# A two-layer encoder trunk on one core: attention in four steps, layer 1's first projections as Strassen-like quads, weights requested later

## The chip, the cores and the metric

The kernel runs on one core of a Trainium2 chip. The metric is the device time of one execution in microseconds (us). Engines: TensorE (PE), VectorE (DVE), ScalarE (ACT), GpSimd (POOL), and SyncE (SP), which here only issues transfers.

## What is computed

Two layers, each with a token mixer of two branches and a feed-forward block, on 1024 tokens of width 1024 in float32:

```python
for layer in range(2):
    hn = rmsnorm(h, norm1_g[layer])
    proj = hn @ w_in[layer]          # u 512, q 512, k 128, v 128, gate_a 1024, gate_b 1024
    y_a = s5_branch(u, ...)          # two-directional S5 scan (32 groups), gelu, z * sigmoid(z @ w_glu)
    y_b = windowed_gqa(q, k, v, ...) # blocks of 128 queries against 3 blocks of keys, a sink logit, T5 bias
    merged = sigmoid(gate_a) * (y_a @ w_branch_a[layer]) + sigmoid(gate_b) * (y_b @ w_branch_b[layer])
    h = h + merged @ w_out[layer]
    hn2 = rmsnorm(h, norm2_g[layer])
    h = h + (silu(hn2 @ w_gate[layer]) * (hn2 @ w_up[layer])) @ w_down[layer]
return rmsnorm(h, final_g)
```

## The kernel before

**Numbers.** Every operand of a large product is split into two float32r parts, `hi` (a cast, on ACT) and `lo` (the rest, a subtraction on DVE). A product of a 128x128 weight block with 512 tokens is three matmuls of PE: hi by hi, hi by lo, lo by hi (`chain`). A weight granule of 128x1024 comes by an SP transfer into one of four `raw` buffers and is then split (`whi` on ACT at L164, `wlo` on DVE at L165). Tokens are in two halves `h` of 512, so a 128-wide output tile of a projection (`proj`, PSUM bank `pj`) is two items of 24 matmuls, one for each half.

**Quads.** The feed-forward block takes gate and up tiles in pairs (`Quad`): sums and differences of the halves of the input (`sums`, `sum_pairs`: tiles `tt0` to `tt3`) and of the weights make seven products do the work of eight. A pair of plain tiles is 96 matmuls, a quad 84.

**Order.** The program is a list of items, `self.seq`, recorded by `build`; an item is a function and the granules it needs. `emit` runs it in order; `ahead` fetches and splits granules ahead of their use: before granule n is split, granules up to n + `R_BUFS` (4) are requested. Engines take instructions in the order of their queues; the order in a stretch of the start is strict, elsewhere a scheduler may move an instruction among its neighbours.

**Layer.** A layer goes through: the norm; projections k, v, q0, q1, u; 16 attention units (2 key heads x 8 blocks); the S5 stage; the gated unit on the S5 output (`glu`); the branches; w_out; the feed-forward block.

- *Attention* (`attention_items`). A unit is: scores into four banks `s` on PE (`att_scores`), with bias and maximum on DVE (`x<-s`, L797) and exponentials on ACT; scaling on DVE (`att_scale`, L814); transposes on PE (`att_transpose`, bank `pt`, L822), copied by ACT to `p`; products with v on PE (`att_values`, bank `pv`). In a loop of 18 steps, step i has the scores and scaling of unit i, the transposes of unit i-1 and the values of unit i-2. Filler items (projections not needed yet: q2, q3 and gate tiles) stand between them, `per` of them to a step: 0.6 in layer 0, 1 in layer 1.
- *S5* (`s5_states`, `s5_output`, `s5_gelu`, `s5_store`). There are 16 states and 8 outputs. A state is 16 matmuls (bank `s5x`), nine instructions of DVE (L949 to L965, four of them one scan each, the last ones make `s5s`), four copies on ACT to `s5sg` (L969). An output `s5y` takes two states; ACT squares and copies it, DVE makes `s5w`, ACT a tanh, DVE `s5g` (L1007), and four transfers take it to `zd` (L1012). Of the 16 states, 6 are made in the last attention steps; the loop of `s5_items` takes the rest, two to an iteration, with `per` fillers: 2.2 in layer 0, 2 in layer 1.
- *glu* (`glu_items`). Loads `z` back from `zd` in token order (L1097), splits it into `zp0` to `zp3`, and multiplies.

In layer 1 the filler list has 42 items: six of u, four of q2 and q3, and 32 of the gates. Its attention takes 20 of them, the S5 loop 18, and four stand between the S5 loop and glu. In layer 0 the fillers of the S5 loop are the seven gate items left by attention and the branch products `br` of attention's output (12 matmuls each).

Of the kernel before, what the change touches and what calls it, by code (L numbers as in the profile page):

```python
# [96 lines left out]
class Trunk:  # L97
# [582 lines left out]
    apart = None  # L680

    def proj(self, l, m, done, xs=None):

        g = self.w_in(l, m)
        apart = self.apart
        st = {}

        def half(h):
            def run(part=None):
                if part != 1:  # L690
                    st[h] = self.PS(f"pj{m}")
                self.chain(st[h], g, 0, (xs or self.hn)[h], part)
                if apart is None and part != 0:
                    done(h, st[h])
            return run
        if apart is not None:
            apart.extend([(lambda: done(0, st[0]),), (lambda: done(1, st[1]),)])
        return [(half(h), g) for h in range(2)]
# [75 lines left out]
    def att_scores(self, l, kv, b):  # L774
# [5 lines left out]
        sm = self.pm.tile([P, 4, 4], F32, tag="sm", name="sm", bufs=3)  # L780
# [85 lines left out]
    def attention_items(self, l, keys, q23, fill, per, tail):  # L866
# [3 lines left out]
        fill = (list(fill[:2]) if l else []) + q23 + list(fill[2 if l else 0:])  # L870
# [15 lines left out]
        for i in range(18):  # L886
            want = min(len(fill), round(per * (i + 1)) + max(0, i - 15))
# [15 lines left out]
            if i in (5, 7):  # L903
# [217 lines left out]

    def w_out_items(self, l):
# [48 lines left out]
    def ffn_items(self, l, fill, head):  # L1171
# [65 lines left out]
        def sums(j):  # L1237

            at = ((j, 0), (j, 1), (j + 4, 0), (j + 4, 1))
            if early:  # L1240
                y11, y12, y21, y22 = (ys.pop(a) for a in at)
            else:
                y11, y12, y21, y22 = (self.A("y") for _ in at)
                for y, (m, h) in zip((y11, y12, y21, y22), at):
                    hi, lo = self.hn2[h][m]
                    V.tensor_tensor(y, hi.bitcast(F32), lo.bitcast(F32), ADD)
            V.tensor_tensor(y11, y12, y11, SUB)
            V.tensor_tensor(y12, y22, y12, SUB)
            V.tensor_tensor(y22, y22, y11, SUB)
            V.tensor_tensor(y21, y21, y22, SUB)  # L1250
            for k, y in enumerate((y11, y22, y12, y21)):
                T[k][j] = (y, None)

        def sum_pairs(j, k):
            T[k][j] = self.split(T[k][j][0], f"tt{k}")

        def quad_items(f):

            q = Quad(self.t["w_gate"][l, f].rearrange("p k c -> p (k c)"), self.t["w_up"][l, f].rearrange("p k c -> p (k c)"))
            b = {}  # L1260

            def product(bank, g, off, xs, start):
                def run():
                    if start:
                        b[bank] = self.PS(f"q{bank}")
                    self.piece(b[bank], g, off, xs(), start)
                return (run, g)

            B = lambda h, a: lambda: self.hn2[h][a:a + 4]
            p = [product("x", q.a, 0, B(0, 0), True), product("y", q.b, HC, lambda: T[1], True),  # L1270
                 product("v", q.b, 0, lambda: T[0], True), product("x", q.a, HC, B(0, 4), False),
                 product("y", q.c, 0, lambda: T[2], False), product("w", q.d, 0, lambda: T[3], True),
                 product("v", q.e, 0, B(1, 4), False)]

# [103 lines left out]
    def build(self):  # L1378
# [31 lines left out]
        for l in range(DEPTH):  # L1410
# [23 lines left out]
            n0, n1 = (self.norm_parts(h, "ra", 2 * l, lambda m, h=h, src=src: src(m, h), lambda: self.hn) for h in range(2))  # L1434
            v1, v2 = self.halves(vc[0])
            loads, states = self.s5_head(l)
            tail_items = {11: pairs[:1] if l == 0 else []}
            for k, (ld, sts) in enumerate(zip(loads, states)):
                a = 18 - 2 * S5_LEAD + k
                tail_items.setdefault(a - 3, []).append(ld)  # L1440
                tail_items.setdefault(a, []).append(sts)
            if l == 0:
# [3 lines left out]
                def squares(h):  # L1446
                    for m in range(KT):
# [3 lines left out]
                va, vb = self.halves(vc[1])  # L1451
                qa, qb = self.halves(qc[1])
                self.add([(start_layer,), kc[0], vc[0], sq[0], kc[1], va, n0[0], sq[1], vb, n0[1], ke[0], ve[0], n1[0], n0[2],
                          qc[0], n0[3], n0[4], qa, n1[1], ke[1], ve[1], qe[0], qb, n0[5], n1[2], qe[1], q1[0], n1[3], scal[0],
# [9 lines left out]
            else:  # L1464

                k1, k2 = self.halves(kc[0])
# [24 lines left out]
            else:  # L1491
                left = self.s5_items(l, left, 2)
# [148 lines left out]
```

## Time and profile before

| | us |
|---|---|
| median of three runs (2645.35 to 2647.42) | 2646.05 |
| the profiled execution | 2647.46 |
| its span | 2645.7 |
| PE busy | 2589.6 |
| DVE busy | 1660.8 |
| ACT busy | 1066.1 |

The profiled execution is read below; its time is 1.4 us above the median and 1.8 us above its own span. "Busy" is the time in which an engine has an instruction in hand; matmuls overlap, so PE's pace is read from the distance between starts, not from the length of one. Stages of the span, by the names of the tiles that PE works on: layer 0's attention runs from about 213 to 372 us; its S5 stage to about 475; its feed-forward block to 1352; layer 1's norm and k, v, q from 1352 to 1412; its attention to 1598; its S5 stage to 1709; a run of fillers, then glu, to about 1765; the rest to 2645.7.

### The profile page before, as it was taken

The numbers are of one execution on the slowest core, as the hardware profiler recorded it, in microseconds if no ns is written. First come the engines' busy times: TensorE is split into PE (matmuls) and PEld (weight loads), VectorE is DVE, ScalarE is ACT, GpSimd is POOL, SyncE is SP. The second block draws the span as 40 slices with busy tenths as digits, with TensorE's granted clock in tenths as the row PEclk, the third lists the DMA queues.
The fourth block names the chain that finished last, engine by engine and source line by source line (L and its number), as shares of the span: only waits on it lengthen the run. The fifth ranks groups of instructions, "written<-read, shape, count | busy, mean of one in ns | idle before, by whom it ended". The sixth has DMA issues, their size and how long they took to land.

```text
span 2645.7 us, 35155 instructions
## 1 busy us (share of the span) xinstructions
PE 2589.6 (98%) x12878; PEld 2108.3 (80%) x12878; DVE 1660.8 (63%) x3333; ACT 1066.1 (40%) x2053; POOL 360.5 (14%) x524
## 2 busy tenths in 40 slices
PE   8999999999999999999999999999999999999997
PEld 6886677887788888888877778888878888888886
DVE  8985877575986745544673576546376644654556
ACT  5336744422443433333344553353235433333332
POOL 0131001000142210121010001100002221122010
PEclk9999999999999999999999999999999999999998
DMA  4353435354273652564332235434315652455253
GB/s 139 127 182 122 146 119 181 115 191 143 60 194 115 124 105 63 112 127 94 99 151 76 88 120 181 145 124 161 127 64 114 133 124 63 91 121 113 60 109 134
DMA packets 157438, 321.36 MB, mean 121 GB/s; under 512 B 20768, under 2 KB 55840, under 8 KB 157264
## 3 DMA queue, kind: packets, MB, share of 16 engines
q1 hardware_dynamic: 106192, 201.68, 23.3%
q0 software_dynamic: 51072, 117.43, 20.4%
q8 instruction: 101, 1.65, 0.3%
q14 instruction: 73, 0.60, 0.1%
HBM read 196.37 MB, written 122.63 MB: 121 GB/s over the span
## 4 chain that ended last, share of the span: by engine, by line
PE 92%; DVE 5%; issue 1%; ACT 1%; DMA 1%; POOL 1%; SPq 0%; DVEq 0%; POOLq 0%; ACTq 0%
PE pj L176 7%; PE pj L177 6%; PE pj L178 6%; PE dn L176 6%; PE dn L177 6%; PE dn L178 6%; PE qy L188 2%; PE qx L188 2%; PE qx L187 2%; PE qv L188 2%; PE qv L187 2%; PE qy L187 2%; PE qv L189 2%; PE qx L189 2%; PE qy L189 2%; PE br L176 2%
## 5 line engine op out<-in xcount | busy, mean ns | idle before, releaser
L165 DVE TENSOR_TENSOR wlo<-raw,whi 128x1024 fp32r<-128x1024 f32 (+3 forms) x210 | 186.6, 889 | 263.3 <-ACT whi L164 252.3
L164 ACT CAST whi<-raw 128x1024 fp32r<-128x1024 f32 (+3 forms) x210 | 164.3, 782 | 372.1 <-PE pj L177 125.0
L176 PE MATMUL pj<-rah,whi 128*128 128x512 f32 x768 | 306.9, 400 | 1.1 <-ACT rah L113 1.0
L177 PE MATMUL pj<-ral,whi 128*128 128x512 f32 x768 | 300.7, 392 | 0.8 <-DVE ral L114 0.8
L178 PE MATMUL pj<-rah,wlo 128*128 128x512 f32 x768 | 300.4, 391 | 0.0
L1218 POOL DMA_DIRECT2D hs<-dx x208 | 179.4, 868 | 846.6 <-ACT dx L1217 724.7
L176 PEld LDWEIGHTS pj<-rah,whi 128*128 128x128 f32 x768 | 144.8, 189 | 35.1 <-issue 2.4
L178 PEld LDWEIGHTS pj<-rah,wlo 128*128 128x128 f32 x768 | 144.8, 189 | 31.0
L177 PEld LDWEIGHTS pj<-ral,whi 128*128 128x128 f32 x768 | 144.9, 189 | 30.0 <-DVE ral L114 1.8
L1217 ACT COPY dx<-dn 128x512 f32<-128x512 f32 x208 | 121.1, 583 | 76.1 <-PE dn L178 75.4
L797 DVE CUSTOM_DVE_ANT_0 x<-s,bias,nsink 128x384 f32<-128x384 f32 (+1 forms) x128 | 67.7, 580 | 65.7 <-PE s L791 65.6
L187 PE MATMUL qx<-rfh,whi 128*128 128x512 f32 x280 | 108.9, 389 | 0.0
L188 PE MATMUL qx<-rfl,whi 128*128 128x512 f32 x280 | 108.9, 389 | 0.0
L189 PE MATMUL qx<-rfh,wlo 128*128 128x512 f32 x280 | 108.9, 389 | 0.0
L969 ACT COPY s5sg<-s5s 64x256 f32<-64x256 f32 x128 | 51.8, 405 | 123.6 <-DVE s5s L964 116.6
L176 PE MATMUL wo<-mgh,whi 128*128 128x512 f32 x256 | 100.0, 391 | 0.0
L178 PE MATMUL wo<-mgh,wlo 128*128 128x512 f32 x256 | 99.7, 389 | 0.0
L177 PE MATMUL wo<-mgl,whi 128*128 128x512 f32 x256 | 99.6, 389 | 0.0
L113 ACT CAST ffah<-ts 128x512 fp32r<-128x512 f32 x35 | 21.7, 621 | 190.1 <-DVE ts L1296 190.1
L176 PE MATMUL dn<-ffbh,whi 128*128 128x512 f32 x232 | 91.4, 394 | 0.0
L177 PE MATMUL dn<-ffbl,whi 128*128 128x512 f32 x232 | 90.6, 390 | 0.0
L177 PE MATMUL dn<-ffal,whi 128*128 128x512 f32 x232 | 90.4, 390 | 0.0
(431 smaller groups left out, 6711.2 us busy)
## 6 DMA issues: line engine op xcount, KB each, us to landing
hs<-dx POOLq DMA_DIRECT2D x208, 256.0 KB, 6.1
raw<-in_w_in SPq DMA_DIRECT2D x52, 512.0 KB
raw<-in_w_gate SPq DMA_DIRECT2D x44, 512.0 KB
raw<-in_w_up SPq DMA_DIRECT2D x44, 512.0 KB
raw<-in_w_down SPq DMA_DIRECT2D x96, 192.0 KB
g<-th POOLq DMA_DIRECT2D x64, 256.0 KB, 2.9
thr<-g SPq DMA_DIRECT2D x64, 256.0 KB
hs<-h POOLq DMA_DIRECT2D x48, 256.0 KB, 2.3
```

Of the source, the lines that this page charges most:

```text
L164: nc.scalar.copy(g.hi[:, :n], g.raw[:, :n])
L165: nc.vector.tensor_tensor(g.lo[:, :n], g.raw[:, :n], g.hi[:, :n].bitcast(F32), SUB)
L176: mm(ps, lhsT=wh, rhs=xh, start=k == 0, stop=False)
L177: mm(ps, lhsT=wh, rhs=xl, start=False, stop=False)
L178: mm(ps, lhsT=wl, rhs=xh, start=False, stop=k == n - 1)
L187: mm(ps, lhsT=wh, rhs=xh, start=start and k == 0, stop=False)
L188: mm(ps, lhsT=wh, rhs=xl, start=False, stop=False)
L189: mm(ps, lhsT=wl, rhs=xh, start=False, stop=k == len(xs) - 1)
L797: V.tensor_tensor_reduce(out=x[:, :n], in0=ps[:, :n], in1=self.bias[hd][:, bo:bo + n], op0=ADD, op1=ALU.min, scale=-1.0, scalar=self.nsink ...
L969: nc.scalar.copy(SG[64 * r:64 * r + 64, g * 256:(g + 1) * 256].rearrange("p (d n) -> p d n", d=2), Sv[64 * g:64 * g + 64, :, r])
L1217: nc.scalar.copy(t, ps)
L1218: nc.gpsimd.dma_start(self.hs[m, h], t, accum_op=ADD)
```

## The change

The main parts of the diff:

```diff
@@ ahead @@
-            self.fetch_to(min(self.split_ + R_BUFS, len(self.order)))
+            g = self.order[self.split_]
+            self.fetch_to(min(self.split_ + (R_BUFS if isinstance(g, QuadPart) else R_BUFS - 1), len(self.order)))
@@ att_scores @@
-        sm = self.pm.tile([P, 4, 4], F32, tag="sm", name="sm", bufs=3)
+        sm = self.pm.tile([P, 4, 4], F32, tag="sm", name="sm", bufs=4)
@@ attention_items @@
-        for i in range(18):
-            want = min(len(fill), round(per * (i + 1)) + max(0, i - 15))
+        for i in range(19):
+            want = min(len(fill), (min(i + 1, 3) + round(0.45 * max(0, i - 2)) if l == 0 else round(per * (i + 1))) + max(0, i - 15))
...
+            if 0 <= i - 3 < 16:
+                self.item(lambda u=i - 3: values(u))
             if 0 <= i - 2 < 16:
-                self.item(lambda u=i - 2: values(u))
+                self.item(lambda u=i - 2: transpose(u))
             if 0 <= i - 1 < 16:
-                self.item(lambda u=i - 1: transpose(u))
-            if i < 16:
-                self.item(lambda u=i: scale(u))
+                self.item(lambda u=i - 1: scale(u))
@@ linear_quads (new; sums, sum_pairs and quad_products are the code of the feed-forward block, now methods) @@
+        for (m1, done1), (m2, done2) in zip(tiles[::2], tiles[1::2]):
+            p, b = self.quad_products(self.t["w_in"][l, m1], self.t["w_in"][l, m2], lambda: self.hn, T)
...
@@ build, layer 0 @@
-                self.add([(start_layer,), kc[0], vc[0], sq[0], kc[1], va, n0[0], sq[1], vb, n0[1], ke[0], ve[0], n1[0], n0[2],
-                          qc[0], n0[3], n0[4], qa, n1[1], ke[1], ve[1], qe[0], qb, n0[5], n1[2], qe[1], q1[0], n1[3], scal[0],
+                self.add([(start_layer,), kc[0], vc[0], sq[0], kc[1], n0[0], sq[1], vc[1], n0[1], ke[0], ve[0], n1[0], n0[2],
+                          qc[0], n1[1], n0[3], ke[1], ve[1], qe[0], n0[4], qc[1], n0[5], n1[2], qe[1], q1[0], n1[3], scal[0],
@@ build, layer 1 @@
-                         [k1, n1[0], k2, v1, n1[1], n1[2], v2, n1[3], n1[4], n1[5], qc[0], ke[0], ve[0], qe[0], kc[1], ke[1],
-                          vc[1], ve[1]] + keys[:2] + [qc[1], qe[1], vals, bias0] + q1 + us[:2])
-                left = self.attention_items(l, keys, q23, us[2:] + gb + ga, 1, tail_items)
+                us = self.linear_quads(l, [lambda i=i: self.tile_u(l, i) for i in range(4)], T)
+                kvq = self.linear_quads(l, [lambda: self.tile_kv(l, M_K, kn), lambda: self.tile_kv(l, M_V, vn),
+                                            lambda: self.tile_q(l, 0), lambda: self.tile_q(l, 1)], T)
...
+                         [a[0], n1[0], a[1], c[0], n1[1], n1[2], c[1], n1[3], n1[4], n1[5], gb[4], *s[:2], gb[1], *s[2:], gb[3], *sp[1], gb[5],
+                          *sp[0], gb[6], *sp[2], gb[7], *sp[3]] + us + kvq[:15] + keys + kvq[15:17] + [vals] + kvq[17:] + [bias0])
+                left = self.attention_items(l, [None] * 4, q23, gb[8:] + ga, 0.9, tail_items)
...
             else:
-                left = self.s5_items(l, left, 2)
+                left = self.s5_items(l, left, 1)
```

So a plain granule is requested when three others, not four, stand before it; the attention loop has 19 steps, with the scaling of unit i-1, the transposes of unit i-2 and the values of unit i-3 in step i; in layer 0's start two halves of v and q are no longer cut and one norm step stands earlier; in layer 1 eight items of gate tiles (four tiles) go ahead, the sums of the normed input are made between them, and u, k with v, and q0 with q1 become four quads. The filler list of layer 1 then has 28 items, of which 0.9 go to an attention step and one to an S5 iteration.

Where rows are shown below they are the instructions in the order in which they stand in one engine's queue. The first place is PE in layer 0's attention: `s` are score banks, `x` the weights after DVE (L797 or L802 makes `x_2668` of `s_2662`, and `x_2657` of `s_2651`), `pt` the transposes. Before:

```order
L791 MATMUL s_2662<-kk00_2114,qn1_677 128x128
...
L822 MATMUL pt_2706<-cst_226,x_2561 128x128
...
L176 MATMUL pj7_2733<-rah_706,whi_2151 128x512
...
L791 MATMUL s_2761<-kk01_2117,qn1_677 128x384
...
L822 MATMUL pt_2801<-cst_226,x_2668 128x128
```

Now:

```order
L796 MATMUL s_2651<-kk00_2112,qn1_650 128x128
...
L827 MATMUL pt_2695<-cst_226,x_2504 128x128
...
L796 MATMUL s_2723<-kk01_2115,qn1_650 128x384
...
L827 MATMUL pt_2763<-cst_226,x_2558 128x128
...
L176 MATMUL pj10_2793<-rah_585,whi_2372 128x512
...
L796 MATMUL s_2829<-kk01_2115,qn1_650 128x384
...
L827 MATMUL pt_2869<-cst_226,x_2657 128x128
```

The transposes of a unit stood behind the scores of the next unit; now they stand behind those of the unit after that, so one more unit's scores, values and transposes lie between a unit's scores and its transposes.

The second place is PE in layer 1's S5 loop, from the output after states 12 and 13 to the end of the loop; each `pj` line is the first of 24 matmuls of a filler, each `s5y` the first of an output. Before:

```order
L983 MATMUL s5y<-s5uk 128x128
...
L941 MATMUL s5x<-s5uk,s5wbt 64x128 x8
L176 MATMUL pj_15560<-rah,whi 128x512
...
L941 MATMUL s5x<-s5uk,s5wbt 64x128 x8
L176 MATMUL pj_15629<-rah,whi 128x512
...
L983 MATMUL s5y<-s5uk 128x128
...
L176 MATMUL pj_15680<-rah,whi 128x512
...
L176 MATMUL pj_15718<-rah,whi 128x512
```

Now, from the output before the last two states:

```order
L988 MATMUL s5y<-s5uk 128x128
...
L946 MATMUL s5x<-s5uk,s5wbt 64x128 x8
L176 MATMUL pj_15993<-rah,whi 128x512
...
L946 MATMUL s5x<-s5uk,s5wbt 64x128 x8
L988 MATMUL s5y<-s5uk 128x128
...
L176 MATMUL pj_16081<-rah,whi 128x512
...
L988 MATMUL s5y<-s5uk 128x128
...
L176 MATMUL pj_16138<-rah,whi 128x512
...
L176 MATMUL glu<-zp0h,whi 128x512
```

An iteration with states had two fillers and has one; outputs without states stand behind one filler instead of two, and behind the last output there is one filler before glu.

The third place is ACT from the last output to glu; `th` is the tanh of a gate tile, `s5g<-s5w` the tanh of the last output, `zp` the split of glu's input. Before:

```order
L988 ACTIVATE s5g<-s5y 128x512
L989 COPY s5yc<-s5y 128x512
L768 ACTIVATE th_15794<-pj_15769 128x512
L1000 ACTIVATE s5g<-s5w 128x512
L164 CAST whi<-raw 128x1024
L768 ACTIVATE th_15832<-pj_15807 128x512
L768 ACTIVATE th_15866<-pj_15841 128x512
L164 CAST whi<-raw 128x1024
L768 ACTIVATE th_15901<-pj_15876 128x512
L113 CAST zp0h<-z_15905 128x512
```

Now:

```order
L993 ACTIVATE s5g<-s5y 128x512
L994 COPY s5yc<-s5y 128x512
L164 CAST whi<-raw 128x1024
L773 ACTIVATE th_16163<-pj_16138 128x512
L1005 ACTIVATE s5g<-s5w 128x512
L113 CAST zp0h<-z_16175 128x512
```

Three fillers less stand between the last output's tanh and the first split of glu's input; the tanh still stands behind the tanh of the filler that follows the output.

## Rows read from the trace of the kernel before

**Rows 1.** The page: span, and part 1, busy time of each engine.

```profile
span 2645.7 us, 35155 instructions
...
PE 2589.6 (98%) x12878; PEld 2108.3 (80%) x12878; DVE 1660.8 (63%) x3333; ACT 1066.1 (40%) x2053; POOL 360.5 (14%) x524
```

**Rows 2.** Timeline of PE, two fillers of layer 1: start, length, instruction.

```profile
1696.84 0.39 PE L176 MATMUL pj<-rah,whi 128*128 128x512 f32 x1
...
1707.04 0.38 PE L983 MATMUL s5y<-s5uk 128*128 128x128 f32 x2
...
1709.63 0.48 PE L176 MATMUL pj<-rah,whi 128*128 128x512 f32 x1
```

**Rows 3.** The page, part 5: a group of the feed-forward quads; last column: idle before.

```profile
L187 PE MATMUL qx<-rfh,whi 128*128 128x512 f32 x280 | 108.9, 389 | 0.0
```

**Rows 4.** Windows: length, busy us of PE, PEld, DVE, ACT, POOL; TensorE clock; DMA.

```profile
213.00:372.00 159.00, 145.89 (x961) 105.47 (x963) 116.94 (x383) 102.05 (x281) 14.76 (x27) 1.00 0.35 118
1598.00:1709.00 111.00, 111.00 (x704) 93.50 (x701) 77.93 (x156) 44.37 (x88) 22.79 (x39) 1.00 0.54 178
...
450.00:475.00 25.00, 19.21 (x112) 16.43 (x111) 19.62 (x42) 12.46 (x26) 4.76 (x8) 0.86 0.25 82
```

**Rows 5.** Waits of PE, 213 to 372 us: total, times, longest.

```profile
PE pt L822 <- DVE x L814: 3.1, 1, 3.1
PE pt L822 <- ACT th L768: 3.0, 1, 3.0
```

**Rows 6.** Timeline of PE at the start.

```profile
40.24 1.87 PE L303 MATMUL psn<-ones,sqa 128*128 128x1 f32 x8 [4.47 <-DVE sqa L294]
```

**Rows 7.** Timeline of DVE, one iteration of layer 1's S5 loop.

```profile
1665.22 0.69 DVE L949 TENSOR_TENSOR s5a<-s5x,s5tb 128x512 f32<-128x512 f32 x1
...
1671.91 0.69 DVE L949 TENSOR_TENSOR s5a<-s5x,s5tb 128x512 f32<-128x512 f32 x1 [1.20 <-PE s5x L941]
...
1677.31 0.68 DVE L999 SCALAR_TENSOR_TENSOR s5w<-s5g,s5yc 128x512 f32<-128x512 f32 x1
1678.44 1.23 DVE L165 TENSOR_TENSOR wlo<-raw,whi 128x1024 fp32r<-128x1024 f32 x1 [0.44 <-ACT whi L164]
1680.67 0.69 DVE L1007 SCALAR_TENSOR_TENSOR s5g<-s5g,s5yc 128x512 f32<-128x512 f32 x1 [1.01 <-ACT s5g L1000]
1681.30 0.69 DVE L949 TENSOR_TENSOR s5a<-s5x,s5tb 128x512 f32<-128x512 f32 x1
```

**Rows 8.** Timeline of ACT in the same iteration.

```profile
1677.36 1.05 ACT L164 CAST whi<-raw 128x1024 fp32r<-128x1024 f32 x1 [4.67 <-PE pj L177]
1678.31 1.68 ACT L969 COPY s5sg<-s5s 64x256 f32<-64x256 f32 x4
1680.01 0.63 ACT L1000 ACTIVATE s5g<-s5w 128x512 f32<-128x512 f32 x1
```

**Rows 9.** Timeline of PE in layer 0's S5 stage.

```profile
447.93 1.10 PE L941 MATMUL s5x<-s5uk,s5wbt 128*64 128x128 f32 x16
448.95 0.50 PE L176 MATMUL br<-ybh,whi 128*128 128x512 f32 x1
...
457.76 1.97 PE L941 MATMUL s5x<-s5uk,s5wbt 128*64 128x128 f32 x16 [5.79 <-DMA s5uk<-ud]
```

**Rows 10.** Timelines of ACT, DVE and SP behind the last S5 output.

```profile
1715.37 0.60 ACT L768 ACTIVATE th<-pj 128x512 f32<-128x512 f32 x1 [4.38 <-PE pj L178]
1715.86 0.62 ACT L1000 ACTIVATE s5g<-s5w 128x512 f32<-128x512 f32 x1
...
1717.24 2.46 SPq L1012 DMA_DIRECT2D zd<-s5g  x4
```

**Rows 11.** All instructions on tile `zd`: issue to landing; those on `z`: duration in ns.

```profile
DMA to landing us min/median/max: 2.0/2.7/5.8
...
L113 ACT CAST zp3h<-z x4: 607/627/635, 499.5 to 1755.2; 128x512 fp32r<-128x512 f32 x4
L114 DVE TENSOR_TENSOR zp3l<-z,zp3h x4: 684/684/693, 500.2 to 1756.1; 128x512 fp32r<-128x512 f32 x4
```

More of the change, by code (lines that the diff above doesn't have):

```diff
@@ L678, in w_in @@
         return Granule(self.t["w_in"][l, m].rearrange("p k c -> p (k c)"), DM)
-    apart = None
+    apart = grab = None
     def proj(self, l, m, done, xs=None):
+        if self.grab is not None:
+            self.grab.append((m, done))
+            return []
         g = self.w_in(l, m)
@@ L869, in attention_items @@
         stage = {}
-        fill = (list(fill[:2]) if l else []) + q23 + list(fill[2 if l else 0:])
+        fill = q23 + list(fill)
         def scores(u):
@@ L902, in attention_items @@
             self.add(tail.get(i, []))
-            if i in (5, 7):
+            if i in (5, 7) and keys[-1]:
                 self.add([keys[(i - 1) // 2]])
@@ L1119, in glu_items, with sums @@
         return early, split, out
+    def sums(self, T, ys, pairs, j):
+        V = self.nc.vector
+        at = ((j, 0), (j, 1), (j + 4, 0), (j + 4, 1))
+        if ys is not None:
+            y11, y12, y21, y22 = (ys.pop(a) for a in at)
+        else:
+            y11, y12, y21, y22 = (self.A("y") for _ in at)
+            for y, (m, h) in zip((y11, y12, y21, y22), at):
+                hi, lo = pairs[h][m]
+                V.tensor_tensor(y, hi.bitcast(F32), lo.bitcast(F32), ADD)
+        V.tensor_tensor(y11, y12, y11, SUB)
+        V.tensor_tensor(y12, y22, y12, SUB)
+        V.tensor_tensor(y22, y22, y11, SUB)
+        V.tensor_tensor(y21, y21, y22, SUB)
+        for k, y in enumerate((y11, y22, y12, y21)):
+            T[k][j] = (y, None)
@@ new lines, in sum_pairs, with quad_products, product, run @@
+    def sum_pairs(self, T, j, k):
+        T[k][j] = self.split(T[k][j][0], f"tt{k}")
+    def quad_products(self, src1, src2, pairs, T):
+        q = Quad(*(s.rearrange("p k c -> p (k c)") for s in (src1, src2)))
+        b = {}
+        def product(bank, g, off, xs, start):
+            def run():
+                if start:
+                    b[bank] = self.PS(f"q{bank}")
+                self.piece(b[bank], g, off, xs(), start)
+            return (run, g)
+        B = lambda h, a: lambda: pairs()[h][a:a + 4]
+        return [product("x", q.a, 0, B(0, 0), True), product("y", q.b, HC, lambda: T[1], True),
+                product("v", q.b, 0, lambda: T[0], True), product("x", q.a, HC, B(0, 4), False),
+                product("y", q.c, 0, lambda: T[2], False), product("w", q.d, 0, lambda: T[3], True),
+                product("v", q.e, 0, B(1, 4), False)], b
@@ L1237, in sums @@
         def sums(j):
[L1239 to L1252, printed above, removed]
+            self.sums(T, ys, self.hn2, j)
         def sum_pairs(j, k):
-            T[k][j] = self.split(T[k][j][0], f"tt{k}")
+            self.sum_pairs(T, j, k)
         def quad_items(f):
[L1259 to L1273, printed above, removed]
+            p, b = self.quad_products(self.t["w_gate"][l, f], self.t["w_up"][l, f], lambda: self.hn2, T)
             def first():
@@ L1433, in build @@
             src = (lambda m, h: xs[h][m]) if l == 0 else (lambda m, h: self.h2[m, h])
-            n0, n1 = (self.norm_parts(h, "ra", 2 * l, lambda m, h=h, src=src: src(m, h), lambda: self.hn) for h in range(2))
+            ys, T = {}, [[None] * 4 for _ in range(4)]
+            n0, n1 = (self.norm_parts(h, "ra", 2 * l, lambda m, h=h, src=src: src(m, h), lambda: self.hn, ys if l else None)
+                      for h in range(2))
             v1, v2 = self.halves(vc[0])
             loads, states = self.s5_head(l)
-            tail_items = {11: pairs[:1] if l == 0 else []}
+            tail_items = {12: pairs[:1] if l == 0 else []}
             for k, (ld, sts) in enumerate(zip(loads, states)):
-                a = 18 - 2 * S5_LEAD + k
+                a = 19 - 2 * S5_LEAD + k
                 tail_items.setdefault(a - 3, []).append(ld)
```

44 lines of the change are left out of this document (41 added, 3 removed).

## The prediction

> **What bounds the kernel now.** I read the page's busy line first [rows 1]: PE has an instruction in hand for 2589.6 of 2645.7 us, so the time is PE's work plus the places where PE waits, about 56 us by that line. Then PE's pace: from 1696.84 to 1707.04 us 45 matmuls of 512 columns start [rows 2], 0.2267 us each, though one lasts 0.39. A filler of 24 is 5.44 us, and the output `s5y` behind it takes 2.6 (1707.04 to 1709.63). So two kinds of edit can pay: fewer matmuls, or fewer waits. A third kind can cost: taking PE work out of a place where it hid another engine. For that I read the windows by stage [rows 4]. In layer 0's attention PE is busy 145.89 of 159 us, so 13.1 us are waits. In layer 1's S5 stage PE is busy all 111 us, so nothing waits there now; DVE is busy 77.9 of them, but not evenly, since only five of its eight outputs stand beside new states. Last come the timelines of DVE, ACT and SP at the places that the change touches.
>
> **Later requests.** In layer 0 and in the feed-forward blocks, SP's queue holds the same transfers in the same order as before, except for one `w_br_b` granule that moves behind six S5 loads. A request waits for the split that frees its buffer, and that is the same split. So I count nothing, also for the largest single wait of layer 0, 5.79 us for an S5 load [rows 9]. If it did go, about 8 us would be gained: the wait and half of some 4.4 us that PE then works at half clock (the window's clock is 0.86 [rows 4]).
>
> **The start.** PE waits 4.47 us for the sum of squares of half 1 [rows 6]. Two splits of a weight (1.2 us each, the length of `wlo` in [rows 7]) no longer stand ahead of these squares on DVE, so the sum can come about 2 us earlier; against it a norm step stands earlier and finds its sum less ready. DVE is the busy engine until half 1 is normed, and its work is not less. I take a gain of 2, between 0 and the 4.47 of the wait.
>
> **Four attention steps, layer 0.** The two largest waits are transposes waiting for DVE's `x` and for ACT to free a bank, 3.1 and 3.0 us [rows 5]. PE's own work for a unit is (145.89 - 13 fillers x 5.44 - 6 `s5x` x 1.02) / 16 = 4.3 us, DVE's (116.94 - 6 states x 5.4 - 7 splits x 1.2) / 16 = 4.8, with its tables. With one more unit between a unit's scores and its transposes, the chain maximum, exponential, scaling has 4.3 us more of PE work to hide behind. What is late next is DVE itself: in a step with a state it has 10.2 us of work, PE 5.3 and a filler of 5.44, and where the filler is missing DVE falls behind. Walking the new order of both queues by hand with these durations leaves waits of 1.2 us near step 12, 2.2 near step 14 and up to 1.5 later. I let 4 of the 13.1 stay, a gain of 9; bounds 6 and 11. In layer 1 nothing much is to be gained, since a filler of 5.44 us stands in nearly each step.
>
> **Quads in layer 1.** Eight tiles become four quads: 8 x 48 = 384 matmuls become 4 x 84 = 336. 48 x 0.2267 = 10.9 us less on PE, all of it on the path, if the quads do not wait. Those of the feed-forward block have no idle time ahead of them [rows 3], and use the same banks and splits. The 16 sums and 16 pair splits that feed them (some 19 us of DVE, 10 of ACT) stand beside the four plain gate tiles, 8 x 5.44 = 43.5 us of PE; I count them at nothing. If that cover failed, the first quad would wait some us for its last pair.
>
> **What these tiles covered elsewhere.** Four gate tiles and the six items of u are gone from the filler list, so the S5 loop of layer 1 has 8 fillers instead of 18. Here the sum is by hand, time 0 at the first output. PE's own work until the last output's end: 8 outputs x 2.6, 7 fillers x 5.44 and ten states x 1.02 [rows 9] = 69.1 us. DVE cannot begin state 6 before its `s5x`, which stands behind one filler and two outputs, at 11.7; state 7 starts at about 18.4. A state takes 5.4 us of DVE (1671.91 to 1677.31 [rows 7]). After each pair comes `s5w`, ACT's tanh and `s5g`. Before, the next state began 3.99 us behind the last one's end (1677.31 to 1681.30), of which 1.2 is a weight split; ACT's own split of 1.05 us and the copies stand ahead of the tanh [rows 8]. Without these splits the gap is about 2.7 us. Nine states, 48.6, four gaps, 10.8, and two weight splits, 2.3, end at 80.1; the copies of `s5sg` end 1.4 us later, and half an output follows: 82.8. So PE waits 82.8 - 69.1 = **13.7 us** in this loop, where it waits for nothing now. With gaps of only 1.6 it is 9.3, with gaps of 4.0 it is 18.9. The weight requests among the S5 loads may move part of the wait ahead (the load of state 13 stands behind one that waits for a split between states 10 and 11), but not change its end.
>
> **Behind the loop** one filler stands before glu, where eight stood, 43.5 us. From that filler's end: th, tanh, `s5g` and the four transfers are all issued after 4.4 us (the filler before ended at about 1715.3; 1717.24 + 2.46 = 1719.7 [rows 10]); landing 2.7, a load of z 0.4 and as much to land as the row for `zd`, about 2, the cast 0.62 and the split 0.69 [rows 11]: 10.8. PE has 23 glu matmuls that don't need the last quarter of z, 5.2 us. So another 5.6 us of waiting; bounds 3 and 8, from the landing's 2.0 and 5.8.
>
> **The clock.** The window with the 5.79 us wait has a granted clock of 0.86 and the one with waits of 3.1 and 3.0 has 1.00 [rows 4, 5, 9]: the long wait was followed by a stretch at 1.2 GHz, the short ones not. 0.14 x 25 = 3.5 us is what a fall can cost. The loop's waits lie ahead of work that DVE delays anyway, so a fall there hides in part; glu's wait is about as long as the one that cost a fall. I take 2 us, bounds 0 and 7 (two falls).
> The Trainium skill speaks against the change here ("TensorE: Matmul & The Clock Gate", section "What's actually happening"): "the default state is throttled, and activity releases the throttle". By it every new long wait would be followed by half speed. With both falls in full the sum would be 5 us higher, by the row's lesson on short waits it stays as it is; the trace agrees only for the long wait.
>
> **Sum.** -10.9 (quads) - 9 (attention) - 2 (start) + 13.7 (S5 loop) + 5.6 (glu) + 2 (clock) = -0.6. The profiled execution's 2647.46 becomes 2646.9; it lies 1.4 above the median, so the forecast is **2645.5 us**: no difference that can be measured. About 0.2%, 5.3 us, is what a measurement of this kernel can tell from no change.
>
> **Rivals.**
> *Slower: the S5 loop is paced by DVE and ACT at gaps of 4.0.* Then the loop costs 18.9, and with glu at 8 and one fall at 3.5, 30.4 against 21.9 of gains: 2646.05 + 8.5 = 2654.5. It decides once loop, glu and clock together exceed 27.2. For it: the 3.99 in the row; against it: half of the gaps have no split ahead of them. Chance 0.26.
> *Faster: the waits are shorter than the walk.* With gaps of 1.6 (9.3), glu 3, no fall, attention 11 and start 3, it is -24.9 + 12.3 = -12.6: 2633.5; half way there is already measurable. For it: DVE's busy time has gaps that a scheduler can fill. Chance 0.26.
> *Faster: the later requests do remove the wait of 5.79 us and its slow stretch:* -8, 2637.5. Against it: SP's queue is the same there. Chance 0.05.
> *By the quoted rule two falls in full:* +5, 2650.5, within the first case's range; chance 0.1, part of it.
> *The four steps do nothing,* since DVE is the bound in layer 0's attention too: the gain of 9 is gone, 2654.5. DVE busy 116.94 of 159 speaks against it. Chance 0.03.
>
> **How the numbers follow.** The forecast case has 0.40 with its neighbourhood of 5.3 us either side (2640.8 to 2651.3). Faster 0.26 + 0.05 = 0.31, and slower 0.26 + 0.03 = 0.29. Cutting about a tenth at each end, the range reaches from 2634 to 2657; within it the forecast case's own is 2641 to 2651.
>
> **What would show it.** Right: layer 1's k, v, q and u as `q` groups of 336 matmuls without idle time; PE waits of 4 us instead of 13.1 in layer 0's attention; in layer 1's S5 loop waits of `s5y` or `s5x` of about 14 us and DVE without idle time from state 7 to 15; a wait of glu of about 5 us for `zp3`; the wait of 5.79 us unchanged. Wrong: an S5 loop in which PE does not wait, or one that waits for loads far beyond DVE; quads waiting for their sums; or a slow stretch behind each wait.

## The result and the profile after

The changed kernel took 2670.22 us (median of 4 runs, 2667.38 to 2671.69), the kernel before 2645.78 beside it (4 runs, 2645.35 to 2647.42): a ratio of 1.0085, 95% interval 1.0072 to 1.0097. That is slower by 24.4 us, outside the forecast range. The profiled execution took 2670.47 us. Its page, span and busy line (as [rows 1]):

```profile
span 2668.7 us, 35161 instructions
...
PE 2592.8 (97%) x12830; PEld 2107.6 (79%) x12830; DVE 1709.0 (64%) x3413; ACT 1084.0 (41%) x2085; POOL 359.5 (13%) x524
```

PE's records became 48 fewer, as the quads promise, yet PE is busy 3.2 us longer: at half clock a matmul is in hand for longer (0.63 us where one of 512 columns otherwise shows 0.39). The mean granted clock of the whole span is 0.987, and was 0.993.

To place the 23.0 us by which the span grew I take both spans between landmarks of PE's work, and call *idle* of a stretch its length less what the same matmuls take at full clock, back to back; it holds waits and slow clock together.

| stretch | idle before | idle after | forecast of the difference | measured |
|---|---|---|---|---|
| start to the first scores | 18.5 | 16.3 | -2 | -2.2 |
| layer 0's attention | 65.7 | 66.0 | -9 | +0.3 |
| layer 1's norm, with the tiles around it (feed-forward block before it included) | 17.6 | 22.4 | 0 | +4.8 |
| quads: 48 matmuls fewer | | | -10.9 | -10.9 |
| layer 1's attention | 53.3 | 58.3 | 0 | +5.0 |
| layer 1's S5 loop, first to last output | 11.7 | 25.8 | +13.7 | +14.1 |
| last output to the end of glu | 0.2 | 10.4 | +5.6, and clock 2 | +10.1 |
| all other stretches | | | 0 | +1.6 |

The measured column adds up to 22.8. (The attention rows hold score and value matmuls that never reach the pace of the long ones, so only their differences mean something.) The windows of these places, as [rows 4]: length, busy us of PE, PEld, DVE, ACT, POOL, then the granted clock.

```profile
211.00:370.00 159.00, 147.16 (x957) 106.37 (x957) 116.32 (x381) 101.29 (x280) 14.77 (x26) 0.99 0.36 117
1673.00:1757.00 84.00, 74.07 (x509) 62.94 (x506) 70.44 (x149) 33.17 (x71) 16.12 (x27) 0.92 0.59 189
448.00:473.00 25.00, 18.91 (x109) 16.11 (x108) 19.63 (x42) 12.28 (x26) 4.75 (x8) 0.86 0.26 82
1340.00:1350.00 10.00, 5.95 (x23) 4.83 (x22) 5.64 (x15) 2.04 (x4) 1.08 (x2) 0.76 0.59 235
1350.00:1360.00 10.00, 10.00 (x42) 8.13 (x41) 8.73 (x15) 4.58 (x8) 1.08 (x2) 0.90 0.14 52
...
1690.00:1710.00 20.00, 15.35 (x102) 12.61 (x101) 17.26 (x38) 7.98 (x17) 3.09 (x6) 0.83 0.79 254
1770.00:1780.00 10.00, 7.71 (x19) 4.99 (x19) 6.49 (x11) 6.55 (x12) 0.00 (x0) 0.57 0.55 186
```

And PE's timeline at each of them; the bracket is the wait just before the instruction and what ended it:

```profile
37.67 1.77 PE L305 MATMUL psn<-ones,sqa 128*128 128x1 f32 x8 [2.12 <-DVE sqa L296]
...
456.23 1.98 PE L946 MATMUL s5x<-s5uk,s5wbt 128*64 128x128 f32 x16 [6.09 <-DMA s5uk<-ud]
...
1346.29 2.08 PE L328 MATMUL psn<-cst,rs 128*128 128x128 f32 x8 [4.05 <-DVE rs L89]
...
1628.39 1.98 PE L946 MATMUL s5x<-s5uk,s5wbt 128*64 128x128 f32 x16 [3.84 <-DVE sm L802]
...
1700.99 1.98 PE L946 MATMUL s5x<-s5uk,s5wbt 128*64 128x128 f32 x16 [4.65 <-ACT s5g L1005]
...
1730.08 1.97 PE L946 MATMUL s5x<-s5uk,s5wbt 128*64 128x128 f32 x16 [5.28 <-DMA s5uk<-ud]
...
1768.06 0.56 PE L176 MATMUL glu<-zp0h,whi 128*128 128x512 f32 x1 [2.43 <-ACT zp0h L113]
...
1774.46 0.79 PE L176 MATMUL glu<-zp2h,whi 128*128 128x512 f32 x1 [2.24 <-ACT zp2h L113]
```

The first row answers to [rows 6]: the wait at the start fell from 4.47 to 2.12. The second answers to [rows 9]: the wait for that S5 load stayed (5.79, now 6.09). Then come six waits that the kernel before did not have at this length.

The quads do not wait for their sums. The groups of two of the products that read sums (`tt2`, `tt3` with `whs`) have no idle time ahead of them; that of the first product, which reads none, waits 1.1 us once, for ACT's copy `qp` (columns as [rows 3]):

```profile
L187 PE MATMUL qx<-rah,whi 128*128 128x512 f32 x32 | 12.6, 392 | 1.1 <-ACT qp L1179 1.1
...
L187 PE MATMUL qy<-tt2h,whs 128*128 128x512 f32 x16 | 6.4, 397 | 0.0
...
L187 PE MATMUL qw<-tt3h,whs 128*128 128x512 f32 x16 | 6.2, 389 | 0.0
```

**Layer 0's attention.** PE's waits from 211 to 370 us, as [rows 5]:

```profile
PE pv L842 <- ACT p L829: 5.7, 6, 1.7
PE s5x L946 <- issue: 2.8, 1, 2.8
PE pt L827 <- ACT th L773: 1.5, 1, 1.5
```

The 3.1 us of a transpose waiting for `x` are gone, as meant. In their place the values wait for ACT's copy `p` of the transposes, six times. ACT's timeline shows why:

```profile
297.03 0.60 ACT L806 ACTIVATE x<-x,sm 128x384 f32<-128x384 f32 x1
...
298.37 0.41 ACT L584 COPY TB<-tt 128x256 f32<-128x256 f32 x1 [0.55 <-DVE sm L816]
298.68 0.50 ACT L586 ACTIVATE TB<-tt 128x128 f32<-128x128 f32 x2
299.09 1.54 ACT L829 COPY p<-pt 128x512 f32<-128x512 f32 x3
```

The transposes ended at 296.6, but the copies begin at 299.09, behind the exponentials of the newest unit and two pieces of an S5 table; PE, which wanted the first of them at 298.18, waits 1.53. The other five waits have the same exponentials ahead of the copies. The change put a unit more between scores and transposes, but none between transposes and values.

All waits of this window together fell only from 13.1 to 11.8 us (159 less PE's 147.16), and the clock took that back. Behind one of them PE works at 1.2 GHz for a while; PE's row, and the window of the 6 us from there:

```profile
324.35 1.85 PE L946 MATMUL s5x<-s5uk,s5wbt 128*64 128x128 f32 x16 [2.75 <-issue]
...
324.00:330.00 6.00, 5.65 (x29) 4.66 (x30) 4.52 (x18) 5.27 (x16) 0.00 (x0) 0.72 0.62 175
```

"issue" means that the profile names nothing that ended the wait; DVE is busy for 5.90 of the 6 us before. At 0.72 these 6 us lose 1.7. The kernel before has 2.37 at the same place, and its window stays at 1.00 [rows 4]. This stretch is no accident of one execution: all nine traces with four attention steps have one between 315 and 331 us, none of the five with three steps has one there.

**Layer 1's norm.** DVE's timeline:

```profile
1341.22 0.36 DVE L89 SCALAR_TENSOR_TENSOR rs<-rs 128x4 f32<-128x4 f32 x2
1344.12 0.69 DVE L139 TENSOR_TENSOR sm<-raw 128x512 f32<-128x512 f32 x1 [2.54 <-DMA raw<-in_w_in]
1344.73 0.15 DVE L89 TENSOR_TENSOR rs<-rs 128x4 f32<-128x4 f32 x1
```

`sm<-raw` is the first weight sum of the u quads, written some thirty items later. The scheduler moved it into the root's chain of small steps (`rs`). Its transfer had not landed, and the chain stood behind it for 2.54 us and its own 0.69; PE's wait for `rs` went from 0.9 to 4.05 us. Together with the 1.1 us for `qp` above this is most of the 4.8 of the table.

**Layer 1's attention.** At 0.9 fillers to a step, step 15 has none (counted from 0); the state's `s5x` then wants a bank that DVE (`sm`, the maximum of the last scores) has not read: 3.84 us. Behind it the clock is 0.92 and 0.91 in the windows 1620 to 1630 and 1630 to 1640, another 1.7 us.

**Last output to the end of glu.** PE's waits here are 2.43, 0.38 and 2.24, together 5.05 us; the clock of 0.84 from 1765 to 1770 and of 0.57 from 1770 to 1780 loses 0.8 and 4.3, another 5.1.

### The profile page after: what moved, and what is told of

The parts are those of the page before. It is cut to its first block, busy times and chain, and to the rows that moved or that the text cites. A ratio compares the mean times of both kernels' runs of the same rounds, so it can differ in the third digit from the quotient of the medians.

```text
span 2668.7 us, 35161 instructions
## 1 busy us (share of the span) xinstructions
PE 2592.8 (97%) x12830; PEld 2107.6 (79%) x12830; DVE 1709.0 (64%) x3413; ACT 1084.0 (41%) x2085; POOL 359.5 (13%) x524
## 4 chain that ended last, share of the span: by engine, by line
PE 88%; DVE 6%; ACT 2%; DMA 2%; issue 1%; SPq 0%; DVEq 0%; ACTq 0%
PE dn L176 6%; PE pj L176 6%; PE dn L177 6%; PE dn L178 6%; PE pj L177 6%; PE pj L178 6%; PE qx L187 3%; PE qx L189 3%; PE qx L188 3%; PE qy L187 3%; PE qv L189 3%; PE qy L189 3%; PE qy L188 3%; PE qv L187 3%; PE qv L188 3%; PE wo L177 2%
## 5 line engine op out<-in xcount | busy, mean ns | idle before, releaser
L165 DVE TENSOR_TENSOR wlo<-raw,whi 128x1024 fp32r<-128x1024 f32 (+3 forms) x202 | 176.7, 875 | 224.9 <-ACT whi L164 219.2
L164 ACT CAST whi<-raw 128x1024 fp32r<-128x1024 f32 (+3 forms) x202 | 155.4, 769 | 335.2 <-PE pj L177 86.7
L176 PE MATMUL pj<-rah,whi 128*128 128x512 f32 x640 | 257.0, 402 | 0.7 <-ACT rah L113 0.7
L177 PE MATMUL pj<-ral,whi 128*128 128x512 f32 x640 | 250.9, 392 | 0.8 <-DVE ral L114 0.8
L178 PE MATMUL pj<-rah,wlo 128*128 128x512 f32 x640 | 250.9, 392 | 0.0
L176 PEld LDWEIGHTS pj<-rah,whi 128*128 128x128 f32 x640 | 121.5, 190 | 31.0 <-issue 5.0
L178 PEld LDWEIGHTS pj<-rah,wlo 128*128 128x128 f32 x640 | 121.1, 189 | 26.2
L177 PEld LDWEIGHTS pj<-ral,whi 128*128 128x128 f32 x640 | 121.5, 190 | 24.9 <-DVE ral L114 1.1
L802 DVE CUSTOM_DVE_ANT_0 x<-s,bias,nsink 128x384 f32<-128x384 f32 (+1 forms) x128 | 67.4, 581 | 60.6 <-PE s L796 60.2
L775 POOL DMA_DIRECT2D g<-th x64 | 35.9, 561 | 412.5 <-ACT th L773 412.4
```

What stands on the lines that cost most here:

```text
L164: nc.scalar.copy(g.hi[:, :n], g.raw[:, :n])
L165: nc.vector.tensor_tensor(g.lo[:, :n], g.raw[:, :n], g.hi[:, :n].bitcast(F32), SUB)
L176: mm(ps, lhsT=wh, rhs=xh, start=k == 0, stop=False)
L177: mm(ps, lhsT=wh, rhs=xl, start=False, stop=False)
L178: mm(ps, lhsT=wl, rhs=xh, start=False, stop=k == n - 1)
L802: V.tensor_tensor_reduce(out=x[:, :n], in0=ps[:, :n], in1=self.bias[hd][:, bo:bo + n], op0=ADD, op1=ALU.min, scale=-1.0, scalar=self.nsink ...
```

## The experiments

Theory: the time went to places where work that hid another engine was taken away (the S5 loop, the stretch behind it, one attention step) and into one moved instruction at the norm, while the four attention steps give nothing, because ACT and DVE pace that stage. Rivals: the four steps or their fill rule cost something themselves; the quads' sums cost wherever they stand; state loads behind weight requests, not DVE, pace the S5 loop. Most runs are one execution each. Seventeen executions of the kernel before on one of the chips went from 2643.6 to 2653.3, so a difference of 3 us between two single times says nothing, and I read the idle of the stretch that an edit touches.

**The old steps** in the changed kernel, with the old rate in layer 0:

```diff
-        for i in range(19):
-            want = min(len(fill), (min(i + 1, 3) + round(0.45 * max(0, i - 2)) if l == 0 else round(per * (i + 1))) + max(0, i - 15))
+        for i in range(18):
+            want = min(len(fill), round(per * (i + 1)) + max(0, i - 15))
...
+                self.item(lambda u=i - 2: values(u))
+                self.item(lambda u=i - 1: transpose(u))
+                self.item(lambda u=i: scale(u))
```

> The changed kernel with the attention loop of before (18 steps: scores and scaling of unit i, transposes of i-1, values of i-2; 0.6 fillers a step in layer 0, 0.9 in layer 1). Theory A (the four steps help, and the thinner fillers of 0.45 a step ate the gain): layer 0's attention, from the first scores to the first S5 output, stays within 2 us of the 153.2 of before, since this is the loop of before. Theory B (DVE and ACT pace the stage, whatever the number of steps): also 153. It is the base for the run with even fillers. In layer 1 the loop took 178.8 before and 183.9 with four steps at 0.9: if the four steps cost the 5 us there, this run gives 179; if the missing fillers do (0.9 a step leaves two steps without), it gives 183 or more.

2655.34. Layer 0's attention took 153.46 us, with four steps 153.50. Where the 15 us came from is elsewhere: a loop of 18 steps leaves two more fillers for the stretch behind the last output, and the idle time from there to the end of glu fell from 10.4 to 1.0 us; layer 1's attention lost 1.6 less. So cover alone removes nearly all that glu lost, and in layer 0's attention the steps make no difference in sum. Layer 1's attention took 171.34 us with those two fillers (10.9 us) less in it, 182.2 like for like: nearer to the 183 that the expectation gives to the missing fillers than to the 179 that it gives to the steps.

**Four steps, old fill rule in layer 0:**

```diff
-            want = min(len(fill), (min(i + 1, 3) + round(0.45 * max(0, i - 2)) if l == 0 else round(per * (i + 1))) + max(0, i - 15))
+            want = min(len(fill), round(per * (i + 1)) + max(0, i - 15))
```

> The changed kernel with the four attention steps, but with 0.6 fillers a step in layer 0, as before, in place of three at once and then 0.45. Theory A (thinner fillers ate the gain): layer 0's attention takes 146 or less, against 153.5. Theory B (DVE and ACT pace the stage): 152 to 155.

2666.49; layer 0's attention took 158.50 us with one filler (5.44) more in it, 153.06 like for like, and has 65.6 us idle against 66.0. The fill rule is not the cause.

**The kernel before with the four steps alone** (the change's loop and fill rule, no quads, no later weights):

> The kernel before with the four attention steps and the new fill rule of layer 0 alone; no quads, no later weight order. Forecast on record (4 us in layer 0's attention, 5 in layer 1's): 2637. Theory now (VectorE and ScalarE pace those stages, the distance from the copy of the weights to the values is unchanged): the attention of layer 0 within 1 us of 153.15 and the whole at 2645 to 2648.

2644.43. Layer 0's attention took 153.23 us (before 153.15), layer 1's had 53.26 idle (before 53.29). Its waits in layer 0:

```profile
PE pv L837 <- ACT p L824: 5.4, 6, 1.7
PE s5x L941 <- issue: 2.8, 1, 2.8
PE pt L822 <- ACT th L768: 1.5, 1, 1.5
```

These are the changed kernel's waits, in a kernel that has nothing else of the change: the wait on `x` turned into waits on `p`. The forecast gain of 9 is not there, and nothing is lost either. (The expectation recalls the forecast as 4 us in layer 0 and 5 in layer 1; the prediction has all 9 in layer 0.) In layer 1 this kernel has four steps with one filler to each and loses nothing, while the changed kernel with the old steps, at 0.9, still loses 3.4 of the 5.0: there the thinner fillers cost, not the steps. That ACT's queue is why layer 0 gains nothing is read from the traces; no run gave the copies `p` an earlier place.

**Raw weights four ahead again:**

```diff
-            self.fetch_to(min(self.split_ + (R_BUFS if isinstance(g, QuadPart) else R_BUFS - 1), len(self.order)))
+            self.fetch_to(min(self.split_ + R_BUFS, len(self.order)))
```

> The changed kernel with raw weights asked for four ahead for plain tiles too. Theory (the later orders are worth the 2.2 us of the start and nothing else of size): first scores 1 to 2 us later, 2671 to 2673. Rival (the later orders delay the raw tiles of the quads at the transition and cost there): 2664 to 2667.

2669.09, first scores at 216.7 us (changed kernel 217.3), norm 22.4 us idle in both. Neither expectation holds: the later requests do nothing, and the 2.2 us at the start come from its new order of items.

**Branch products as cover.** The twelve-matmul products of attention's output go into layer 1's S5 loop, 2.2 to an iteration, and the split that they need goes into attention, as layer 0 has it (the lines that placed both later go):

```diff
-            tail_items = {12: pairs[:1] if l == 0 else []}
+            tail_items = {12: pairs[:1]}
...
                 left = self.attention_items(l, [None] * 4, q23, gb[8:] + ga, 0.9, tail_items)
+                self.add(pairs[1:])
...
-                left = self.s5_items(l, left, 1)
+                left = self.s5_items(l, left + bb, 2.2)
```

> The changed kernel with the sixteen products of attention's output with w_br_b as fillers of layer 1's S5 loop too, at 2.2 a step of the loop as in layer 0 (the split of that output moves into the attention loop). Theory 1 (the loop and glu lost the PE work that hid DVE and a chain of transfers): PE waits in the loop and for glu fall from about 24 us to under 4, and the time to about 2646. Rival (the loop is paced by loads and by DVE however much PE work there is): waits of over 10 us stay, the time is above 2656.

2653.25. The loop's idle time fell from 25.8 to 12.6 us (before: 11.7), and PE is never without work in its middle, at full clock:

```profile
1650.00:1700.00 50.00, 50.00 (x302) 40.89 (x301) 30.32 (x63) 21.78 (x41) 6.32 (x11) 1.00 0.47 155
1700.00:1740.00 40.00, 40.00 (x259) 33.65 (x259) 27.58 (x56) 15.25 (x30) 7.86 (x13) 1.00 0.52 170
```

Behind it 5.9 us stay, 2.7 of them the last output waiting for ACT's copy of its state, and glu waits 0.2. So what the loop and glu lost is cover. The time stays above the 2646 of the theory: those 5.9 us, the norm and the attention of layer 1 are not mended by this edit.

**No filler in the loop:** its fillers stand behind the last output, ahead of glu.

```diff
-                left = self.s5_items(l, left, 1)
+                left = self.s5_items(l, left, 0)
```

> No filler at all in the S5 loop of layer 1; its twelve products go behind the last output, in front of the glu tiles. Theory (VectorE's chain of eight iterations sets the length of the loop once the fillers are few): the loop from the first to the last output gets shorter by 3 us at most, those for the splits of the fillers' weights, against 20 us of filler work taken out, so that its idle time on TensorE grows from 25.8 to 42 or more; the glu waits vanish (about -9.5), and the sum is 2675 to 2680. Rival (state loads that wait on SP's queue behind weight requests set the loop): without weights asked for in the loop it shortens by 14 to 20 us, its idle time falls to 12 to 20, and the sum is 2650 to 2658.

2689.62, above the ranges of both. The expectation has an error of mine: the loop holds seven filler items of 5.44 us, 38 us of work, not twelve of 20. The row of the first instructions of the outputs (duration, first and last start), of the kernel before:

```profile
L983 PE MATMUL s5y<-s5uk x64: 270/275/377, 1599.4 to 1709.2; 128*128 128x128 f32 x64
```

of the changed kernel:

```profile
L988 PE MATMUL s5y<-s5uk x64: 270/275/377, 1673.6 to 1759.5; 128*128 128x128 f32 x64
```

and without fillers:

```profile
L988 PE MATMUL s5y<-s5uk x64: 275/377/583, 1671.4 to 1748.7; 128*128 128x128 f32 x64
```

From the first output to the last it is 109.8 us before, 85.9 in the changed kernel and 77.3 without fillers: 38 us of PE's work out, 8.6 us shorter. That is more than the 3 that I gave the theory and less than the rival's 14. DVE's timeline without fillers decides:

```profile
1681.41 0.69 DVE L1012 SCALAR_TENSOR_TENSOR s5g<-s5g,s5yc 128x512 f32<-128x512 f32 x1 [0.69 <-ACT s5g L1005]
...
1694.95 0.69 DVE L1012 SCALAR_TENSOR_TENSOR s5g<-s5g,s5yc 128x512 f32<-128x512 f32 x1 [1.46 <-ACT s5g L1005]
...
1708.50 0.69 DVE L1012 SCALAR_TENSOR_TENSOR s5g<-s5g,s5yc 128x512 f32<-128x512 f32 x1 [1.46 <-ACT s5g L1005]
...
1749.13 0.69 DVE L1012 SCALAR_TENSOR_TENSOR s5g<-s5g,s5yc 128x512 f32<-128x512 f32 x1 [1.46 <-ACT s5g L1005]
```

Five iterations of 13.54 us, with no weight split between them, and no wait but 1.46 for ACT's tanh: DVE's two states and their gelu are the floor of an iteration. The changed kernel's rows have the same step where no split stands between:

```profile
1700.98 0.69 DVE L1012 SCALAR_TENSOR_TENSOR s5g<-s5g,s5yc 128x512 f32<-128x512 f32 x1 [1.45 <-ACT s5g L1005]
...
1714.53 0.69 DVE L1012 SCALAR_TENSOR_TENSOR s5g<-s5g,s5yc 128x512 f32<-128x512 f32 x1 [1.46 <-ACT s5g L1005]
```

So state loads don't pace the loop: PE's two long waits in the changed kernel (4.65 and 5.28) fall at loads that stand behind weight requests on SP's queue, but DVE's only waits from 1693 to 1756 us are the four for the tanh and 1.0 for a split's `hi`. Of the 8.6 us, some 2.5 are two splits of the fillers' weights (these rows start at 1683.68, 1700.98, 1714.53, 1729.44, 1742.99 and 1757.69 in the changed kernel: 14.91 and 14.70 where the others have 13.55), 3.8 the first iteration (17.30), whose states stand behind fillers, and the rest lies behind the last of them. Without fillers glu still waits 2.1 us for `zp3`, where the expectation had nothing.

**The written order at the norm**, first for DVE, ACT and PE over fifty items:

```diff
+                r0 = len(self.seq) + len(tail) - 6
                 self.add(tail[:-6] + [n0[0]] + tail[-6:-4] + [n0[1], n0[2], tail[-4], n0[3], tail[-3], n0[4], tail[-2], n0[5],
...
+                self.strict = set(self.strict) | set(range(r0, r0 + 50))
```

> The changed kernel with DVE, ACT and PE held to the written order from the last w_down products of layer 0 through the layer-1 norm to the sums, so that the first weight sum of a quad no longer stands inside the norm's chain on DVE. Theory 1 (that sum waited 2.5 us for its weights at the head of DVE's queue, the norm came late and the clock fell): the stretch from layer 0's first feed-forward product to layer 1's first scores is 4 to 5 us shorter, 835.5 instead of 840.1. Rival (the norm waits for its residual loads anyway, DMA being full at that place): within 1 us of 840.

2672.97: the wait for `rs` is gone, but PE in the written order waits 9.2 us for half 1's squares; norm and quads have 25.2 us idle.

**The same for DVE alone:**

```diff
-                    strict = self.tc.manual_schedule(engines=IN_ORDER)
+                    strict = self.tc.manual_schedule(engines={mybir.EngineType.DVE} if i in late else IN_ORDER)
...
+                self.late = range(r0, r0 + 50)
```

> VectorE's instructions stay in the written order over the norm of layer 1 (fifty items), so that the first weight sum of the u quads cannot stand ahead of the root's chain; TensorE and ScalarE stay free. Theory (the hoisted weight sum and its wait for a raw transfer cost the 4.8 us that the stretch around the norm lost): about 2666, 4 to 5 us below the changed kernel, with the wait of the row norm's matrix gone back to about 1 us. Rival (the quads' longer list of VectorE work there costs it wherever it stands): 2670 to 2672.

2669.66, 22.8 us idle: `rs` no longer waits, but in the written order each sum of squares stands behind its residual and DVE waits 0.70 for ACT's square, six times; the normed tiles come later, and PE waits 0.3 to 1.0 us for them five times over and works at 1.2 GHz for part of the time:

```profile
1350.00:1360.00 10.00, 7.07 (x20) 4.06 (x20) 8.28 (x14) 3.67 (x7) 1.08 (x2) 0.74 0.14 52
1360.00:1370.00 10.00, 9.69 (x35) 7.67 (x34) 3.79 (x14) 1.07 (x2) 1.09 (x2) 0.57 0.31 107
```

By its numbers the rival had won, but the edit had brought waits of its own; so I confined it.

**DVE in order from the nineteenth item on:** up to the norm's first products its queue is that of the changed kernel without the two sums.

```diff
-                self.late = range(r0, r0 + 50)
+                self.late = range(r0 + 18, r0 + 50)
```

> VectorE in the written order from the nineteenth item of the transition on, so that its order up to the norm's first products is that of the changed kernel but for the two weight sums, which now stand behind them. Theory (the first sum's wait for its transfer costs the transition): the wait for the root in front of the row norm falls from 4.05 us to about 1, and the two stretches around it lose 4 to 5 us together: 2665 to 2667. Rival (the sum's work costs wherever it stands, as the strict order over fifty items read): 2669 to 2671.

2665.09, 16.2 us idle against 22.4. PE's row, where 4.05 stood:

```profile
1342.24 1.16 PE L329 MATMUL psn<-cst,rs 128*128 128x128 f32 x8 [0.94 <-DVE rs L89]
```

The theory holds for the wait: the moved sum was its cause, since its work now stands behind the norm and makes no wait there. Only half of the 6.2 us is that wait, however; the last section has the rest.

**Steps, rates and cover together:** the cover above with the old three attention steps and the old rule in layer 0, one filler to a step in layer 1 and 2.6 to an S5 iteration.

> The run with second-branch products as fillers in layer 1's S5 loop, with the three attention steps of before, one filler per step in layer 1 and 2.6 fillers per iteration in the loop. Theory (the layer-1 attention lost 5 us to a step without filler, the loop's end lost 3 us for want of fillers): 2646 to 2650. Rival (the four steps were worth something, and the losses are the quads' own): 2653 or more.

2646.48. Layer 1's attention has 54.5 us idle instead of 58.3: its 3.84 us wait is gone. With DVE in order over fifty items:

> The same with VectorE in the written order over the norm of layer 1. If both theories hold, 2641 to 2645, just below the kernel before; if the strict order gives nothing, as the run beside it.

2648.80 against 2647.71 of before beside it, ratio 1.0003 (0.9993 to 1.0013). And with the sums confined as in the run of 2665.09:

> The run with three steps, one filler per step and branch products in the loop, with the weight sums behind the norm as in the run beside it. Theory: 4 to 5 us below that run's 2646.5, so 2641 to 2643, faster than the kernel before by 3 to 5. Rival: 2646 to 2647, the same as before.

2645.36 (12 runs) against 2647.06 (17 runs), ratio 0.9993 (0.9985 to 1.0002): all that was lost is back, but no gain is shown. Of the 10.9 and 2.2 us saved, 11.1 are still given back, by the idle times of its profile against before: 4.7 in the S5 loop (16.4), 1.6 at the norm (19.2), 1.5 in layer 0's attention (67.2), 1.3 in layer 1's (54.6) and 2.0 from the last output to the end of glu (2.3). The remaining 2.0 is within what its 12 and 17 executions can't tell from nothing; the 2641 to 2643 of the theory are missed.

## Why the prediction was wrong, step by step

- *Quads, -10.9:* right. 48 matmuls fewer, no wait at their sums, one of 1.1 us for `qp`.
- *Start, -2:* right in size (2.2) and place (the sum of squares, 4.47 to 2.12).
- *Later requests, nothing:* right; the run without them is the same. (The S5 load's 5.79 us is not layer 0's largest wait: PE's first matmul waits 7.3 us, in both kernels.)
- *S5 loop, +13.7:* right, 14.1, and for the reason given: two states of 5.4 and a gap of 2.7 are 13.5 to an iteration, and the runs show 13.54. That the size fits so well is partly luck. From the first output's start to the last one's end took 86.3 us where the hand sum has 82.8, and the loop of before without seven fillers, 110.3 - 38.1, is 72.2 where it has 69.1 for PE's own work: both terms are 3 us low, and their difference is not. Of the 14.1, PE's two waits are 9.9; the rest is slow clock (0.92 in the window).
- *Layer 0's attention, -9:* this step failed, and it is the largest error: +0.3. Waits of 11.8 us stay, not 4. "What is late next is DVE itself" missed what came next: ACT, whose copies `p` stand behind the newest exponentials (5.7 of the 11.8). The wait of 2.75 that the profile gives no cause for may still be DVE's; the clock behind it took 1.7. The rival "the four steps do nothing" had 0.03 for a wrong reason: I asked whether DVE was full, and not whether the next hand-over in the chain had become any longer. The run with the four steps alone is 0.08 us from before in that stage.
- *glu, +5.6:* right in cause, and the waits come to 5.05, though for `zp0` and `zp2` and not, as I counted, for the last quarter `zp3`.
- *Clock, +2, bounds 0 and 7:* this term failed by its size. It is 5.1 at glu alone, and 1.7 in each layer's attention, 8.5 us at these three places. The lesson on short waits was drawn from two windows; the same trace has a fall behind waits of 1.04 and 0.79 (last section).
- *Not in the sum at all:* the norm (+4.8, of which the moved weight sum is 3.1 and `qp` 1.1) and the attention step without filler (+5.0, with its slow clock). "I count them at nothing" asked only whether the quads would wait for their sums, and not what their first weight sum, free to move, could stand in front of. And "a filler stands in nearly each step" passed over the steps that have none at 0.9, 4 and 15, of which the second cost.

The quoted rule of the Trainium skill ("TensorE: Matmul & The Clock Gate", section "What's actually happening") had the better of it: the waits of 4.05, of 3.84, of 4.65 and of glu were each followed by a stretch at half speed, and so was one of 2.75. Waits of about 1 us were not always, and in the kernel before the waits of 3.1 and 3.0 were not [rows 4, 5].

## What to carry to other kernels

When work is removed from the path, list what it was hiding, place by place, down to the single loop step that stays empty; here 10.9 us of PE's work saved cost some 34 us of cover, order and slow clock. When a stage is stretched by one step, follow the whole chain of hand-overs: here the wait moved to the next one, which had no more distance than before. And where a scheduler may move instructions, ask of each new one that waits for a transfer what it can be moved in front of.

## What the runs showed of the chip

The same waits were not always followed by the same clock. The kernel with all edits together has the same waits at the norm as the run of 2665.09: 0.95 and 0.94 for `rs`, then 1.04 for the first normed tile's `rah` in both and 0.80 and 0.79 for its `ral`. Its windows:

```profile
1350.00:1360.00 10.00, 8.17 (x34) 6.08 (x33) 9.77 (x16) 4.62 (x8) 1.29 (x3) 0.96 0.28 105
1360.00:1370.00 10.00, 10.00 (x41) 8.48 (x40) 3.48 (x15) 1.89 (x4) 0.54 (x1) 0.70 0.08 28
```

and those of the run of 2665.09:

```profile
1350.00:1360.00 10.00, 8.17 (x39) 6.10 (x37) 9.17 (x15) 4.47 (x8) 1.09 (x2) 1.00 0.23 87
1360.00:1370.00 10.00, 10.00 (x50) 8.44 (x50) 7.19 (x20) 3.81 (x7) 1.08 (x2) 1.00 0.15 54
```

One fell to 1.2 GHz for a part of these windows and the other did not, which is 3.4 us (0.04 and 0.30 of 10). The kernel before, with waits of 0.9, 1.04 and 0.79, fell there as well:

```profile
1350.00:1360.00 10.00, 8.17 (x35) 6.00 (x33) 10.00 (x17) 4.75 (x9) 1.54 (x3) 0.99 0.28 105
1360.00:1370.00 10.00, 10.00 (x40) 8.47 (x39) 3.25 (x15) 1.08 (x2) 0.00 (x0) 0.67 0.01 2
```

and the changed kernel lost the same 3.4 from 1340 to 1360 (0.76 and 0.90), behind its 4.05. So of the 6.2 us by which the confined order lowered the idle time, 3.1 are the wait that went (4.05 to 0.94), and about as much is what the clock gave in that execution. With all edits together, and the fall, the stretch has 19.2 us against 17.6 before, of which the wait for `qp` is 1.1. Executions can differ by that much at such a place.
